# Turning the upper gate frames on VectorE from quarter loads, and adding the gated embedding on GpSimd, in a one-core streaming encoder layer

## The chip, the cores and the metric

The kernel runs on one core of one Trainium2 chip. The metric is the device time of one execution in microseconds (us), taken as a median over runs. The engines are TensorE (PE; its weight loads are PEld), VectorE (DVE), ScalarE (ACT), GpSimd (POOL) and SyncE (SP, which here only issues DMAs). Each engine works through its own queue in order; between queues, semaphores make one instruction wait for another.

## The reference

One layer on 2048 prompt frames and 32 sample frames of 1024 channels, in float32. Cut to what matters:

```python
hn = rmsnorm(h, g_mix)
proj = hn @ w_in                                   # 1024 x 3072
...                                                # yA: gated short convolution, yB: multi-scale pooling
h = h + jnp.concatenate([yA, yB], axis=-1) @ w_out
gate = jax.nn.sigmoid(rmsnorm(h, g_ple) @ w_ple_gate)
h = h + (p @ w_ple) * gate
return rmsnorm(h, g_final)
```

The change concerns the last three lines, the gate stage. The states of the mixers are outputs too; the change does not touch them.

## The kernel before

**Numbers.** Each float32 operand of a matrix product is split into a high part, rounded to the format that PE multiplies (a cast on ACT, L81), and the rest (a subtraction on DVE, L84; the low half). A product is then three matmuls per slice of 128 channels: high by high, high by low, low by high.

**Tiles and products.** Frames come in tiles of 128: tiles 0 to 15 are the prompt, tile 16 is the short tile of 32 sample frames. The gate stage works on pairs of tiles (i, i+1), i = 0, 2, ... 14; "pair 8" is tiles 8 and 9. The even tile is the upper one, the odd the lower. For each pair `seven` (L273) makes seven block products of 12 matmuls each (L185), in three PSUM banks `x_g`, `y_g`, `z_g`, from seven prepared operands: `11` and `12` (the two channel halves of the upper frames), `22`, and the combinations `S1` to `S4` of upper and lower frames. It stands in a scheme of Strassen's kind, so that seven products do the work of eight. The first product of a pair reads `g{i}_11`, the second `g{i}_12`; the last reads `g{i}_22`.

**Preparing a pair.** PE needs the frames with channels on partitions, and `h_d` in DRAM has frames on partitions. `prep_g` makes the operands of pair i+2 while PE works on pair i, in steps that are put between the products of pair i. The *lower* frames are loaded by `by_quarters` (L1512): four DMAs, one per quarter of the channels, each with rows of 1 KB, so that one DVE `STREAM_TRANSPOSE` in place (`turned_here`, L1560) turns the tile. The *upper* frames are loaded whole by one DMA (`load_rows`, L396), brought into another order by two ACT copies `ho` (L1552), and turned by eight PE transposes into a PSUM bank `pth` (L1554); the split and the combinations then read `pth`. `comb` (L1743) adds or subtracts two halves on DVE; `put` splits them.

**After each product.** `gate_ops`: a half of the gate is copied out of PSUM by ACT (`c_g`, L1573), completed by a DVE addition (L1581), put through the sigmoid by ACT (L1582; for the last product of a pair straight from PSUM into `g_g`, L1579), multiplied into the embedding tile `e` by DVE (L1584) and added to `h` by DVE (L1585). There are four such halves in a pair: two for each tile.

**Finishing a tile.** `done_g`: ACT squares and sums `h` (L94, output `junk`), POOL makes the mean (`ms_f`, L73) and its inverse root (`rstd_f`, L77), DVE scales `h` (L1592), and a DMA stores it (L1593, on POOL's queue up to tile 5 and for the short tile, on SP's queue from tile 6). The tiles of pair 12 and before all end so. The last pair is done by `last_pair`, which has an order of its own that is partly written out (`keep_in_program_order`); `done_g(13)` stands within it.

**What sets the order.** Each engine's queue is made by the framework's scheduler from the program's order and the dependences, except for instructions that are kept in program order. A change in what an operation depends on or runs on may thus move others.

The names in the change: `ya`, `xh` are rings of 128x1024 tiles, `ss` and `cmb` rings of smaller ones, `ring4` takes a tile of such a ring, `tiles[i]` gives first row and number of rows, `whole` is a strided view that fits the layout of a tile turned in place.

Of the kernel before, what the change touches and what calls it, by code (L numbers as in the profile page):

```python
# [15 lines left out]
P = 128  # L16
# [20 lines left out]
def trunk(ctx, tc, x_p, x_s, c_conv, c_pool, p_p, p_s, g_mix, w_in, conv_w, conv_b, pool_w,  # L37
# [344 lines left out]
    def ring4(t, name):  # L382
        return t.tile([P, D], F32, tag="t", name=name)
# [920 lines left out]
    with ExitStack() as s2:  # L1304
# [199 lines left out]
        tops, _ = rows_of_weight(ya, "wg_t", g_d, 0)  # L1504
        weight_slot(W, "wg", *PLACES[0])
        weight_parts(W, tops, None, "11", "T1")
        def by_quarters(i):

            r, n = tiles[i]
            t = ring4(ya, f"hn_{i}")  # L1510
            for q in range(4):
                nc.sync.dma_start(t[q * 32:q * 32 + 32].rearrange("p (g c) -> p g c", g=4),  # L1512
                                  h_d[r:r + P, q * 256:q * 256 + 256].rearrange("(g p) c -> p g c", p=32))
            return t
# [13 lines left out]
            bots = rows_of_weight(cmb, "wg_b", g_d, 1, range(2))[0]  # L1528
        with tc.issue_after(embed_weight.ins):
            bots += rows_of_weight(cmb, "wg_b", g_d, 1, range(2, KH))[0]  # L1530
            first_h = load_rows(xh, "hn", 0, h_d)

        rest_e = [*range(EARLY, NT - 2), NT - 1]

# [33 lines left out]
        def gate_ops(h, e, n, name, i):  # L1568
            scale = lambda at: rs_h[:n, i + at[0]:i + at[0] + 1]

            def carry(ps, at):
                t = st.tile([P, NH], F32, tag="t", name=f"c_{name}_{at[0]}{at[1]}")
                carried.append(nc.scalar.copy(t[:n], ps[:n]))  # L1573
                return t

            def out(ps, c, at):
                if c is None:
                    c = st.tile([P, NH], F32, tag="t", name=f"g_{name}_{at[0]}{at[1]}")
                    nc.scalar.activation(c[:n], ps[:n], AF.Sigmoid, scale=scale(at))  # L1579
# [4 lines left out]
                nc.vector.tensor_tensor(ee, ee, c[:n], op=ALU.mult)  # L1584
                nc.vector.tensor_tensor(hh, hh, ee, op=ALU.add)  # L1585

            return carry, out

# [24 lines left out]
        def last_pair(i, A, before):  # L1613
# [118 lines left out]
        def prep_g(i, ahead=False):  # L1732
# [26 lines left out]

            def second():  # L1760
                a21, a22 = lower
                s1 = comb("S1", a21, a22, ALU.add, whole)
# [3 lines left out]
                s3 = comb("S3", whole(a11), a21, ALU.subtract, whole)  # L1766
                put("12", a12)
                put("S2", s2)
                s4 = comb("S4", a12, s2, ALU.subtract)
                put("S1", s1)  # L1770
                put("S3", s3)
                put("S4", s4)
                put("22", a22, whole)

            S[i] = A
# [73 lines left out]
```

## Time and profile before

| | before |
|---|---|
| time, median of 3 runs | 916.7 us (914.71 to 917.25) |
| the profiled execution | 913.25 us |
| its span, first to last instruction | 911.5 us |
| mean granted PE clock | 0.998 |
| PE busy | 894.6 us (98%) |
| DVE busy | 702.9 us (77%) |
| ACT busy | 460.6 us (51%) |
| POOL busy | 149.8 us (16%) |

Times are us from the start of the span unless marked ns. A row of the timeline gives start, length, engine, line, operation, output <- input, the count where several are joined, and in brackets the idle time of that engine just before, with the one that ended it. In rows by groups, busy time and mean length stand behind the first bar, idle time behind the second. The gate stage begins at about 690 us: up to about 732 us PE still makes embedding products, then come the pairs; PE's last matmul ends at 903.77 us.

### The profile page before, as it was taken

The numbers are of one execution on the slowest core, as the hardware profiler recorded it, in microseconds if no ns is written. First come the engines' busy times: TensorE is split into PE (matmuls) and PEld (weight loads), VectorE is DVE, ScalarE is ACT, GpSimd is POOL, SyncE is SP. The second block draws the span as 40 slices with busy tenths as digits, with TensorE's granted clock in tenths as the row PEclk, the third lists the DMA queues.
The fourth block names the chain that finished last, engine by engine and source line by source line (L and its number), as shares of the span: only waits on it lengthen the run. The fifth ranks groups of instructions, "written<-read, shape, count | busy, mean of one in ns | idle before, by whom it ended". The sixth has DMA issues, their size and how long they took to land.

```text
span 911.5 us, 12171 instructions
## 1 busy us (share of the span) xinstructions
PE 894.6 (98%) x4174; PEld 722.5 (79%) x4174; DVE 702.9 (77%) x1158; ACT 460.6 (51%) x834; POOL 149.8 (16%) x290
## 2 busy tenths in 40 slices
PE   8999999999999999999999999999999999999996
PEld 6788888878888887877778887888788888778885
DVE  6899789797993697846667579965666988897885
ACT  7744555455443345533344366544434865565554
POOL 2210121222122114100000020121111211120012
PEclk9999999999999999999999999999999999999999
DMA  8255296748599767567746495887777975575554
GB/s 268 61 187 179 76 269 191 217 151 262 151 328 422 212 201 216 199 216 236 256 129 199 162 318 200 260 245 257 212 267 256 325 257 174 184 237 185 184 192 167
DMA packets 113387, 198.52 MB, mean 218 GB/s; under 512 B 13174, under 2 KB 70062, under 8 KB 112429
## 3 DMA queue, kind: packets, MB, share of 16 engines
q1 hardware_dynamic: 91309, 124.72, 42.5%
q0 software_dynamic: 19568, 68.62, 22.5%
q10 hardware_dynamic: 2448, 4.39, 1.3%
q8 instruction: 33, 0.54, 0.2%
q14 instruction: 29, 0.24, 0.1%
HBM read 132.53 MB, written 65.15 MB: 217 GB/s over the span
## 4 chain that ended last, share of the span: by engine, by line
PE 54%; issue 11%; DMA 10%; DVE 2%; POOL 1%; ACT 1%; POOLq 0%; ACTq 0%; DVEq 0%
PE x_g L185 9%; PE x_o L185 7%; PE z_g L185 5%; DMA raw_zab_0b<-in_w_in_dram 4%; PE x_zab L646 4%; PE x_zbv L646 3%; PE z_o L185 3%; PE x_ch L646 3%; PE y_g L185 2%; PE z_zab L646 2%; PE y_o L185 2%; DMA B<-p_d 2%; PE e L109 2%; PE z_ch L646 1%; PE z_zbv L646 1%
## 5 line engine op out<-in xcount | busy, mean ns | idle before, releaser
L185 PE MATMUL z_o<-wo,y_S 128*128 128x512 f32 x192 | 47.4, 389 | 0.0
L646 PE MATMUL x_zab<-B,w_zab_S 128*128 128x512 f32 x192 | 46.9, 393 | 0.4 <-DVE w_zab_S L84 0.2
L185 PE MATMUL x_o<-wo_T,y_S 128*128 128x512 f32 x192 | 46.3, 390 | 0.6 <-DVE c_o L1319 0.6
L185 PE MATMUL z_g<-wg,g_S 128*128 128x512 f32 x192 | 46.8, 391 | 0.0
L646 PE MATMUL z_zab<-B,w_zab_S 128*128 128x512 f32 x192 | 46.7, 391 | 0.0
L185 PE MATMUL x_o<-wo,y 128*128 128x512 f32 x192 | 45.2, 389 | 0.0
L646 PEld LDWEIGHTS x_zab<-B,w_zab_S 128*128 128x128 f32 x192 | 35.7, 188 | 9.4 <-DVE w_zab_S L84 0.6
L185 PEld LDWEIGHTS x_o<-wo_T,y_S 128*128 128x128 f32 x192 | 35.9, 188 | 8.4 <-DVE c_o L1319 1.0
L185 PEld LDWEIGHTS x_o<-wo,y 128*128 128x128 f32 x192 | 36.1, 188 | 7.7
L646 PEld LDWEIGHTS z_zab<-B,w_zab_S 128*128 128x128 f32 x192 | 35.8, 188 | 7.8 <-DVE w_zab_S L84 0.3
L185 PEld LDWEIGHTS z_o<-wo,y_S 128*128 128x128 f32 x192 | 36.1, 188 | 7.5
L646 PE MATMUL x_ch<-B,w_ch_S 128*128 128x512 f32 x168 | 41.9, 392 | 0.0
L185 PEld LDWEIGHTS z_g<-wg,g_S 128*128 128x128 f32 x192 | 35.8, 188 | 7.5 <-ACT c_g L1573 0.2
L646 PE MATMUL z_ch<-B,w_ch_S 128*128 128x512 f32 x168 | 40.5, 390 | 1.1 <-ACT U L986 1.1
L646 PE MATMUL x_zbv<-B,w_zbv_S 128*128 128x512 f32 x168 | 40.9, 392 | 0.3 <-ACT zs L986 0.3
L646 PE MATMUL z_zbv<-B,w_zbv_S 128*128 128x512 f32 x168 | 40.4, 390 | 0.0
L646 PEld LDWEIGHTS z_ch<-B,w_ch_S 128*128 128x128 f32 x168 | 31.5, 188 | 8.1 <-ACT U L986 1.6
L646 PEld LDWEIGHTS x_zbv<-B,w_zbv_S 128*128 128x128 f32 x168 | 31.3, 188 | 8.1 <-ACT zs L986 0.8
L646 PEld LDWEIGHTS x_ch<-B,w_ch_S 128*128 128x128 f32 x168 | 31.3, 188 | 7.3 <-ACT U L986 0.4
L646 PEld LDWEIGHTS z_zbv<-B,w_zbv_S 128*128 128x128 f32 x168 | 31.5, 188 | 6.5
L81 ACT CAST y_S<-y_fS 128x512 fp32r<-128x512 f32 x28 | 17.0, 619 | 28.1 <-PE x_o L185 12.2
L1319 DVE TENSOR_TENSOR c_o<-x_o,x 128x512 f32<-128x512 f32 x14 | 9.7, 689 | 22.6 <-PE x_o L185 22.6
(552 smaller groups left out, 2285.0 us busy)
## 6 DMA issues: line engine op xcount, KB each, us to landing
wn<-in_w_in_dram SPq DMA_DIRECT2D x24, 512.0 KB, 4.7
y<-y_d SPq DMA_DIRECT2D x16, 512.0 KB, 6.5
p_dT<-T POOLq DMA_DIRECT2D x15, 512.0 KB, 5.2
e<-e_d SPq DMA_DIRECT2D x15, 512.0 KB, 5.0
x<-in_x_prompt_dram SPq DMA_DIRECT2D x14, 512.0 KB, 4.9
B<-p_d POOLq DMA_DIRECT2D x3, 2048.0 KB, 16.8
B<-p_dT POOLq DMA_DIRECT2D x3, 2048.0 KB, 22.8
h_d<-x SPq DMA_DIRECT2D x12, 512.0 KB, 6.3
```

Of the source, the lines that this page charges most:

```text
L81: ins = nc.scalar.copy(hi, src)
L109: nc.tensor.matmul(ps, pps[:, a, k], wp[k][b][:, cs], start=k + q == 0, stop=k == 1 and q == 2)
L185: nc.tensor.matmul(ps[:n], lhs[:, k, a, :n], w[b][:, k], start=start and k + q == 0, stop=k == KH - 1 and q == 2, skip_group_check=True)
L646: nc.tensor.matmul(ps, lhs[:, k, x], b[:, k, y], start=start and k + q == 0, stop=stop and k == KH - 1 and q == 2, skip_group_check=True)
L1319: add = lambda o, a, b: nc.vector.tensor_tensor(o, a, b, op=ALU.add)
```

## The change

Three edits, all in the gate stage:

1. The upper frames are loaded by quarters as the lower ones are (those of pair 0 too, into the ring `xh`), and turned in place by DVE. The copies `ho`, the PE transposes and `pth` are gone for tiles 0, 2, ... 14; the short tile keeps them. Splits and combinations read strided SBUF views.
2. The last addition of the gate, `h += e * gate`, runs on POOL for full tiles (28 additions) and stays on DVE for the short tile.
3. `last_pair` gets a `drain` on POOL, kept in program order. It stands in POOL's queue behind `rstd_f12` and ahead of `ms_f13`.

```diff
-        def by_quarters(i):
+        def by_quarters(i, pool=ya):
             r, n = tiles[i]
-            t = ring4(ya, f"hn_{i}")
+            t = ring4(pool, f"hn_{i}")
...
-            first_h = load_rows(xh, "hn", 0, h_d)
+            first_h = by_quarters(0, xh)
...
-                nc.vector.tensor_tensor(hh, hh, ee, op=ALU.add)
+                (nc.gpsimd if n == P else nc.vector).tensor_tensor(hh, hh, ee, op=ALU.add)
...
+            fixed(nc.gpsimd.drain())
...
-            def comb(q, x, y, op, view=lambda t: t):
-                t = ss.tile([P, KH, P], F32, tag="s", name=f"g{i}_f{q}")
-                nc.vector.tensor_tensor(view(t), x, y, op=op)
+            def comb(q, x, y, op):
+                t = whole(ss.tile([P, KH, P], F32, tag="s", name=f"g{i}_f{q}"))
+                nc.vector.tensor_tensor(t, x, y, op=op)
...
-                got["upper"] = load_rows(ya, "hn", i, h_d) if i else first_h
+                got["upper"] = by_quarters(i) if i else first_h
...
-                a11, a12 = turned(i, got["upper"])
-                put("11", a11)
+                a11, a12 = turned_here(got["upper"])
+                put("11", a11, whole)
```

The other `put` and `comb` lines change in the same way. Lines behind the drain are two higher in the changed kernel (`comb` is L1745 there). The rows of the queues below show what that does to the order at three places. In the names, `g10_11` is operand `11` of pair 10, `hn_10` its upper frames, `e_8`, `h_8` the embedding and the frames of tile 8, `c_g8_01` and `g_g8_10` the gate halves of pair 8; the number behind is the buffer's.

**From pair 8 to pair 10.** DVE's queue before, around the end of pair 8:

```order
L1581 TENSOR_TENSOR c_g8_01_7415<-z_g8_7364,c_g8_01_7415 128x512
L84 TENSOR_TENSOR g10_S4_7454<-g10_fS4_7446,g10_S4_7454 128x4x128
L84 TENSOR_TENSOR g10_22_7457<-hn_11_7395,g10_22_7457 128x4x128
L1584 TENSOR_TENSOR e_9_7360<-e_9_7360,c_g8_11_7472 128x512
L1584 TENSOR_TENSOR e_8_7358<-e_8_7358,c_g8_01_7415 128x512
L1585 TENSOR_TENSOR h_9_7356<-h_9_7356,e_9_7360 128x512
L1585 TENSOR_TENSOR h_8_7354<-h_8_7354,e_8_7358 128x512
L1584 TENSOR_TENSOR e_9_7360<-e_9_7360,g_g8_10_7518 128x512
L1585 TENSOR_TENSOR h_9_7356<-h_9_7356,e_9_7360 128x512
L1581 TENSOR_TENSOR c_g10_00_7561<-y_g10_7547,c_g10_00_7561 128x512
L1592 TENSOR_SCALAR h_8_7354<-h_8_7354,rstd_f8_7526,g_bc_89 128x1024
L1592 TENSOR_SCALAR h_9_7356<-h_9_7356,rstd_f9_7534,g_bc_89 128x1024
```

DVE's queue of the changed kernel at the same place:

```order
L1581 TENSOR_TENSOR c_g8_01_7368<-z_g8_7314,c_g8_01_7368 128x512
L1745 TENSOR_TENSOR g10_fS1_7370<-hn_11_7345 128x512
L1584 TENSOR_TENSOR e_8_7308<-e_8_7308,c_g8_01_7368 128x512
L1584 TENSOR_TENSOR e_9_7310<-e_9_7310,g_g8_10_7458 128x512
L1592 TENSOR_SCALAR h_8_7304<-h_8_7304,rstd_f8_7466,g_bc_89 128x1024
L1560 STREAM_TRANSPOSE hn_10_7350<-hn_10_7350 128x1024
L1592 TENSOR_SCALAR h_9_7306<-h_9_7306,rstd_f9_7474,g_bc_89 128x1024
L84 TENSOR_TENSOR g10_11_7373<-hn_10_7350,g10_11_7373 128x4x128
L1745 TENSOR_TENSOR g10_fS2_7376<-g10_fS1_7370,hn_10_7350 128x512
L1745 TENSOR_TENSOR g10_fS3_7378<-hn_10_7350,hn_11_7345 128x512
L84 TENSOR_TENSOR g10_12_7380<-hn_10_7350,g10_12_7380 128x4x128
```

Before, the low half of `g10_11` stood nine places ahead of the first of these rows; now it stands behind the multiplication by `g_g8_10` and the two scalings L1592, and the transpose of `hn_10` has come between those. On POOL's queue of the changed kernel, the additions of pair 8 and what ends tiles 8 and 9:

```order
L1585 TENSOR_TENSOR h_8_7304<-h_8_7304,e_8_7308 128x512
L1585 TENSOR_TENSOR h_9_7306<-h_9_7306,e_9_7310 128x512
L1585 TENSOR_TENSOR h_8_7304<-h_8_7304,e_8_7308 128x512
L1585 TENSOR_TENSOR h_9_7306<-h_9_7306,e_9_7310 128x512
L73 TENSOR_SCALAR ms_f8_7464<-ssq_f8_7462 128x1
L77 TENSOR_TENSOR rstd_f8_7466<-ms_f8_7464,nhalf_83 128x1
L73 TENSOR_SCALAR ms_f9_7472<-ssq_f9_7470 128x1
L77 TENSOR_TENSOR rstd_f9_7474<-ms_f9_7472,nhalf_83 128x1
```

Only the last four of these stood there before. On PE's queue, the first product of pair 10 (12 matmuls) and two matmuls of its second stood ahead of the last product of pair 8; now they stand behind it.

**From pair 10 to pair 12.** ACT's queue before:

```order
L1552 COPY ho_12_0_7604<-hn_12_7584 128x512
L1552 COPY ho_12_1_7611<-hn_12_7584 128x512
L81 COPY g12_11_7617<-pth_12_0_7603 128x4x128
L81 COPY g12_12_7624<-pth_12_1_7610 128x4x128
L81 COPY g12_S2_7627<-g12_fS2_7620 128x4x128
L81 COPY g12_S1_7632<-g12_fS1_7601 128x4x128
L81 COPY g12_S3_7635<-g12_fS3_7622 128x4x128
```

ACT's queue of the changed kernel:

```order
L1582 ACTIVATE c_g10_11_7586<-c_g10_11_7586,rs_h_88 128x512
L1582 ACTIVATE c_g10_01_7542<-c_g10_01_7542,rs_h_88 128x512
L94 ACTIVATE junk_90,ssq_f10_7636<-h_10_7478 128x1024
L81 COPY g12_11_7547<-hn_12_7524 128x4x128
L81 COPY g12_12_7554<-hn_12_7524 128x4x128
L81 COPY g12_S2_7557<-g12_fS2_7550 128x4x128
```

The square of tile 10 (`ssq_f10`) stood behind the casts of pair 12, and now stands ahead of the first of them.

**From pair 12 to pair 14.** DVE's queue of the changed kernel around the end of pair 12:

```order
L1581 TENSOR_TENSOR c_g12_01_7716<-z_g12_7662,c_g12_01_7716 128x512
L1584 TENSOR_TENSOR e_12_7656<-e_12_7656,c_g12_01_7716 128x512
L1584 TENSOR_TENSOR e_13_7658<-e_13_7658,g_g12_10_7806 128x512
L1560 STREAM_TRANSPOSE hn_14_7698<-hn_14_7698 128x1024
L1592 TENSOR_SCALAR h_12_7652<-h_12_7652,rstd_f12_7814,g_bc_89 128x1024
L84 TENSOR_TENSOR g14_11_7721<-hn_14_7698,g14_11_7721 128x4x128
```

And before, in the same part of the program:

```order
L84 TENSOR_TENSOR g14_11_7801<-pth_14_0_7787,g14_11_7801 128x4x128
L1743 TENSOR_TENSOR g14_fS2_7804<-g14_fS1_7785,pth_14_0_7787 128x512
L1743 TENSOR_TENSOR g14_fS3_7806<-pth_14_0_7787,hn_15_7763 128x512
L84 TENSOR_TENSOR g14_12_7808<-pth_14_1_7794,g14_12_7808 128x4x128
L84 TENSOR_TENSOR g14_S2_7811<-g14_fS2_7804,g14_S2_7811 128x4x128
L84 TENSOR_TENSOR g14_S1_7816<-g14_fS1_7785,g14_S1_7816 128x4x128
L84 TENSOR_TENSOR g14_S3_7819<-g14_fS3_7806,g14_S3_7819 128x4x128
L1743 TENSOR_TENSOR g14_fS4_7814<-pth_14_1_7794,g14_fS2_7804 128x512
L1585 TENSOR_TENSOR h_12_7722<-h_12_7722,e_12_7726 128x512
L1584 TENSOR_TENSOR e_13_7728<-e_13_7728,g_g12_10_7886 128x512
L84 TENSOR_TENSOR g14_S4_7822<-g14_fS4_7814,g14_S4_7822 128x4x128
L84 TENSOR_TENSOR g14_22_7825<-hn_15_7763,g14_22_7825 128x4x128
```

The low half of `g14_11` stood ahead of the last multiplication of pair 12 (by `g_g12_10`); now it stands behind it, the transpose of `hn_14` and the scaling of `h_12`.

More of the change, by code (lines that the diff above doesn't have):

```diff
@@ L1761, in second @@
                 a21, a22 = lower
-                s1 = comb("S1", a21, a22, ALU.add, whole)
-                a11, a12 = turned(i, got["upper"])
-                put("11", a11)
+                s1 = comb("S1", a21, a22, ALU.add)
+                a11, a12 = turned_here(got["upper"])
+                put("11", a11, whole)
                 s2 = comb("S2", s1, a11, ALU.subtract)
-                s3 = comb("S3", whole(a11), a21, ALU.subtract, whole)
-                put("12", a12)
-                put("S2", s2)
+                s3 = comb("S3", a11, a21, ALU.subtract)
+                put("12", a12, whole)
+                put("S2", s2, whole)
                 s4 = comb("S4", a12, s2, ALU.subtract)
-                put("S1", s1)
-                put("S3", s3)
-                put("S4", s4)
+                put("S1", s1, whole)
+                put("S3", s3, whole)
+                put("S4", s4, whole)
                 put("22", a22, whole)
```

## The prediction, made before the changed kernel was run

> **What bounds the kernel now.** I begin with the head of the page, then the table of windows over the last stage, the only one in which the order of instructions changes.
>
> ```profile
> span 911.5 us, 12171 instructions
> PE 894.6 (98%) x4174; PEld 722.5 (79%) x4174; DVE 702.9 (77%) x1158; ACT 460.6 (51%) x834; POOL 149.8 (16%) x290
> ```
>
> TensorE (PE) is busy for 98% of the span. The windows below give, for each stretch, its length and then the busy time of PE, of the weight loads, of VectorE (DVE), ScalarE (ACT) and GpSimd (POOL).
>
> ```profile
> 745.00:770.00 25.00, 25.00 (x118) 20.50 (x116) 20.64 (x31) 14.13 (x26) 3.24 (x7) 1.00 0.50 162
> 770.00:795.00 25.00, 25.00 (x119) 20.05 (x118) 20.73 (x33) 13.08 (x25) 3.90 (x7) 1.00 0.55 181
> 795.00:820.00 25.00, 25.00 (x115) 18.76 (x114) 23.25 (x36) 15.35 (x28) 4.99 (x9) 1.00 0.66 215
> 820.00:845.00 25.00, 25.00 (x116) 20.75 (x115) 19.78 (x31) 12.67 (x23) 1.98 (x4) 1.00 0.49 177
> 845.00:870.00 25.00, 25.00 (x115) 20.57 (x114) 20.35 (x30) 14.63 (x26) 2.81 (x6) 1.00 0.50 176
> 870.00:890.00 20.00, 20.00 (x92) 16.17 (x91) 16.35 (x25) 9.96 (x20) 2.70 (x4) 1.00 0.62 221
> ```
>
> From 745 to 890 us PE has no gap at the full clock. So whatever leaves PE's queue there shortens the kernel by its length, and whatever PE waits for lengthens it by the wait. DVE is idle for 145 − 121.1 = 23.9 us of these 145 us: it is not the bound, but it is not far from it.
>
> **What goes: the transposes on PE.** The chain of waits runs over all eight groups for the upper frames (start, length):
>
> ```profile
> 721.68 0.87 PE pth L1554 x8
> ...
> 834.65 0.87 PE pth L1554 x8
> ...
> 857.11 1.03 PE pth L1554 x8
> ...
> 879.68 1.11 PE pth L1554 x8
> ```
>
> The first six take 0.87 or 0.88 each, the last two are longer: with the six, 5.23 + 1.03 + 1.11 = **7.4 us**, all on the path. (The short tile's two groups stay.) The other costs of this edit, by groups (busy us, mean ns):
>
> ```profile
> L1552 ACT COPY ho<-hn 128x512 f32<-128x512 f32 x16 | 9.3, 619 | 5.3 <-DMA hn<-h_d 5.3
> L1560 DVE STREAM_TRANSPOSE hn<-hn 128x1024 f32<-128x1024 f32 x8 | 9.9, 1237 | 0.1
> L1585 DVE TENSOR_TENSOR h<-h,e 128x512 f32<-128x512 f32 x28 | 18.7, 683 | 0.3
> L1646 POOL TENSOR_TENSOR hg<-h,g_bc 128x512 f32<-128x512 f32 x1 | 1.3, 1310 | 0.1
> ```
>
> ACT loses 9.3 us of copies; it is half idle, so that gains nothing by itself. DVE gets eight more transposes (9.9 us) and gives 28 additions to POOL (18.7 us), 8.8 us less in sum, beside a full PE: nothing by itself. POOL gets 28 additions. The nearest row on POOL, a product of two SBUF tiles of the same size, took 1.31 us, against 0.68 on DVE; so 28 × 1.31 = 36.7 us, on an engine that is 16% busy. What counts is who waits for these additions.
>
> **What is added: waits in queues.** The pair boundary 8→10 before shows every hand-off:
>
> ```profile
> 841.25 0.62 ACT L81 CAST g<-hn 128x512 fp32r<-128x512 f32 x1
> ...
> 841.53 2.88 PE L185 MATMUL x_g<-wq,g 128*128 128x512 f32 x12
> ...
> 842.35 0.68 DVE L84 TENSOR_TENSOR g<-hn,g 128x512 fp32r<-128x512 f32 x1
> ...
> 844.45 0.69 ACT L1579 ACTIVATE g_g<-x_g,rs_h 128x512 f32<-128x512 f32 x1 [1.35 <-PE x_g L185]
> ...
> 845.36 0.68 DVE L1584 TENSOR_TENSOR e<-e,g_g 128x512 f32<-128x512 f32 x1
> ...
> 846.77 0.19 POOL L73 TENSOR_SCALAR ms_f<-ssq_f 128x1 f32<-128x1 f32 x1 [19.47 <-ACT junk L94]
> ...
> 846.93 1.06 ACT L94 ACTIVATE junk<-h 128x1024 bf16<-128x1024 f32 x1 [0.25 <-DVE h L1585]
> ...
> 848.17 0.79 POOL L73 TENSOR_SCALAR ms_f<-ssq_f 128x1 f32<-128x1 f32 x1 [0.58 <-ACT junk L94]
> ...
> 849.04 0.55 POOL L77 TENSOR_TENSOR rstd_f<-ms_f,nhalf 128x1 f32<-128x1 f32 x1
> 849.62 1.28 DVE L1592 SCALAR_TENSOR_TENSOR h<-h,rstd_f,g_bc 128x1024 f32<-128x1024 f32 x1 [0.71 <-POOL rstd_f L77]
> ```
>
> Pair 8's last product ends at 841.53 + 2.88 = 844.41 us, and the sigmoid starts 0.04 later. A hand-off to POOL costs about 0.08 (ACT's 846.93 + 1.06 and its 0.19 of accumulator read, then 848.17), POOL to DVE 0.03. The whole tail of pair 8 lies beside PE, which runs on with pair 10, whose `g10_11` was made long before. In the changed order it isn't. DVE's queue now has, ahead of the low half of `g10_11`, which PE's next product reads: the multiplication by `g_g8_10`, the scaling of `h_8`, the transpose of `hn_10` and the scaling of `h_9`. And POOL's queue has the last addition to `h_9`, which needs that multiplication, ahead of the `rstd_f8` that the scaling of `h_8` waits for. So a closed chain through five in-order queues starts when PE finishes pair 8, and PE can't begin pair 10 until it is through. With E the end of PE's last product of the pair: sigmoid E+0.03 to 0.72; multiplication to 1.44; POOL's addition 1.53 to 2.84; `ms_f8` to 3.11, `rstd_f8` to 3.74; scaling of `h_8` 3.77 to 5.05; transpose to 6.24; ACT's cast to 6.87, DVE's scaling of `h_9` beside it to 7.45; the low half to 8.1. The first two matmuls run on the high half, the other ten (0.227 us each, from 2.72 us for twelve without a gap) after 8.1: the product ends at 10.4 in place of 2.72. **Stall at 8→10: 7.7 us.**
>
> *10→12.* On ACT, the square of `h_10` stands ahead of the cast of `g12_11`, and it waits for POOL's second addition to `h_10`. The z product that opens this ends one product (2.72 us) ahead of E: addition to `c_g10_01` to E−2.0, sigmoid to −1.27, multiplication to −0.55, POOL to +0.85, square and accumulator read 0.95 to 2.1, cast to 2.75. **Stall 2.8 us.**
>
> *12→14.* Here the transpose stands ahead of the scaling of `h_12`, but the low half of `g14_11` stands behind that scaling. The same walk to 5.05, low half to 5.7, ten matmuls to 8.0 against 2.72. **Stall 5.3 us.**
>
> *Earlier pairs.* At 4→6 the transpose of `hn_6` stands behind the multiplication by the gate and ahead of the scaling of `h_4`; the short tile's products, which stand on PE between these pairs, cover most, but its own addition in DVE's queue stands behind all that: 1.1 us, at most 2.7. At 6→8 only the transpose stands between: 0.3, at most 1.5. At 0→2 and 2→4 the order leaves the casts ahead of the waits: 0.
>
> *Loads by quarters.* Two DMA rows: 432 packets of such quarters in a window of 4.6 us, and 420 of whole rows in 5.0 us (packets, MB, share of 16 engines' time).
>
> ```profile
> q1 hardware_dynamic: 432, 0.39, 29.2%
> ...
> q1 hardware_dynamic: 420, 1.56, 86.1%
> ```
>
> A quarter packet takes 0.292 × 4.6 × 16 / 432 = 0.050 us, a 4 KB one 0.861 × 5.0 × 16 / 420 = 0.164; 512 per frame against 128 make 1.6 us of the 16 engines against 1.3. This matters once, for the first upper frames, which are loaded while the DMAs are full and PE waits for `pps`:
>
> ```profile
> 690.00:722.00 32.00, 31.72 (x143) 26.00 (x142) 26.30 (x43) 20.90 (x40) 7.94 (x16) 1.00 0.92 328
> 715.97 5.71 PE L109 MATMUL e<-wq,pps 128*128 128x512 f32 x24 [0.28 <-DMA pps<-pp_d]
> ```
>
> I take 0.3 us (0 to 2, since three more issues on SP's queue may also delay the load behind them). Later quarters land in time: the windows above have DMA at 0.49 to 0.66. The **drain** stands in POOL's queue between `rstd_f12` and `ms_f13`; the row of `rstd_f` gives 0.55 us to wait for, which would lie beside PE: 0, and up to about 3 us if it waited for more than the instruction ahead of it.
>
> **Sum.** Stalls 7.7 + 2.8 + 5.3 + 1.1 + 0.3 + 0.3 = 17.5; minus 7.4 saved: +10.1. On the profiled execution's 913.25 us (span 911.5) this gives 923.4; the median of the runs stands 3.45 higher, so **926.8 us**.
>
> **Rivals.** *A, the other side: the saving alone.* If the transposed frames of the next pair are there before each pair's last product ends, as the copies and casts were before, no boundary stalls, and the time is 916.7 − 7.4 = 909 us. For it: PE has no gap now, and DVE has less to do. Against it: the queue order that I walked. It decides at 7.4 us of stalls in sum: only if two of the three big ones didn't happen would the kernel be faster. Chance 0.09.
>
> *B, GpSimd and VectorE hold each other up.* These rows start within 0.05 us of each other; the same small POOL operation took 0.19 above:
>
> ```profile
> 808.40 1.23 DVE L1592 SCALAR_TENSOR_TENSOR h<-h,rstd_f,g_bc 32x1024 f32<-32x1024 f32 x1
> 808.45 1.24 POOL L73 TENSOR_SCALAR ms_f<-ssq_f 128x1 f32<-128x1 f32 x1 [0.39 <-ACT junk L94]
> ```
>
> So POOL waits for a DVE operation with two SBUF inputs. No row shows the reverse. If it holds, each addition may keep DVE for 1.31 us, 36.7 in all, against DVE's idle 23.9 plus the 8.8 that it gives away: about what it has. One addition more in the way at each of seven boundaries is 7 × 1.31 = 9.2, so 936 us; half of that, 931. The multiplications, the low halves and now the S1 to S4 combinations are all of that kind. But in the three long chains DVE itself waits while POOL adds, so most of the collisions fall into its idle time. Chance 0.17.
> [...]
>
> *C, the stalls are about half as long,* because POOL's addition costs what DVE's does and PE's covers are larger than I walked: 8.7 − 7.4 = +1.3, so 918, about no change. Chance 0.10, half of it within 0.3%.
>
> **How the numbers follow.** The forecast (921 to 931) has 0.60, B 0.17, C 0.10, A 0.09, still slower 0.04. To leave no more than 2 in 10 out, the range goes from C's slower half at 918 to above B's 936: 918 to 938. A measurement of this kernel tells 0.3%, 2.75 us, from no change; faster by more has A's 0.09, within it 0.05, slower 0.86.
>
> **What would show it.** PE idle ahead of the first products of pairs 10, 12 and 14, by about 7.7, 2.8 and 5.3 us, released by DVE's low half (10 and 14) and ACT's cast (12); DVE's L1592 waiting for `rstd_f` and that for L1585 on POOL, 28 rows of about 1.31 us; `pth` only for the short tile. PE without gaps there would refute me and mean A. DVE rows far above 0.7 us beside POOL's additions would mean B; a shorter addition or an earlier sigmoid, C.

## The result and the profile after

| | before | changed |
|---|---|---|
| time, median | 915.71 us (4 runs, 914.32 to 917.25) | 942.47 us (4 runs, 941.55 to 948.2) |
| profiled execution | 913.25 us | 948.2 us |
| span | 911.5 us | 946.4 us |
| mean granted PE clock | 0.998 | 0.982 |

The changed kernel takes 1.031 times as long, 95% interval 1.0289 to 1.033: 26.8 us slower, where 10.1 were forecast, and above the range. The profiled execution is the slowest of its four; its trace has 34.9 us more span to explain. One execution of the kernel before, timed beside runs 9 to 11, took 2320 us and is left out of the median given for it there. Head of the page of the changed kernel:

```profile
span 946.4 us, 12072 instructions
...
PE 902.7 (95%) x4110; PEld 722.6 (76%) x4110; DVE 700.7 (74%) x1138; ACT 454.0 (48%) x818; POOL 189.1 (20%) x318
```

PE has 64 matmuls fewer and is busy 8.1 us longer. Two things need to be found: where PE waits, and why its work takes longer. The windows over the gate stage of the changed kernel show both (columns as before; PEclk is the granted clock, behind the five busy times):

```profile
745.00:770.00 25.00, 21.55 (x89) 17.40 (x88) 14.70 (x21) 12.02 (x21) 7.83 (x9) 0.93 0.66 194
...
795.00:820.00 25.00, 21.76 (x82) 13.96 (x81) 17.60 (x25) 9.17 (x16) 7.56 (x10) 0.86 0.67 203
...
845.00:870.00 25.00, 17.63 (x70) 13.77 (x69) 16.58 (x22) 9.65 (x18) 8.12 (x10) 0.86 0.53 166
...
905.00:920.00 15.00, 10.34 (x34) 7.57 (x33) 11.70 (x16) 6.08 (x10) 4.94 (x5) 0.77 0.36 134
```

Where PE filled every window before, at clock 1.00, these four have gaps and a granted clock of 0.77 to 0.93. The gaps of PE between pairs, from the timeline (in brackets the idle time ahead, and who ended it):

```profile
759.35 4.51 PE L185 MATMUL x_g<-wq,g 128*128 128x512 f32 x12 [3.45 <-DVE c_g L1581]
808.26 0.73 PE L185 MATMUL x_g<-wg,g 128*128 128x512 f32 x2 [1.20 <-ACT g L81]
810.18 1.07 PE L185 MATMUL x_g<-wg,g 128*128 128x512 f32 x2 [1.19 <-DVE g L84]
812.10 1.97 PE L337 MATMUL x_gl<-wg,gl_a 128*64 128x512 f32 x4 [0.84 <-DVE c_gl L1601]
835.38 0.73 PE L185 MATMUL x_g<-wg,g 128*128 128x512 f32 x2 [0.74 <-ACT g L81]
837.60 4.16 PE L185 MATMUL x_g<-wg,g 128*128 128x512 f32 x10 [0.97 <-DVE g L84]
865.00 4.74 PE L185 MATMUL x_g<-wg,g 128*128 128x512 f32 x12 [7.37 <-ACT g L81]
888.67 1.05 PE L185 MATMUL x_g<-wg,g 128*128 128x512 f32 x2 [2.58 <-ACT g L81]
913.14 1.22 PE L185 MATMUL x_g<-wg,g 128*128 128x512 f32 x2 [3.52 <-ACT g L81]
915.51 4.45 PE L185 MATMUL x_g<-wg,g 128*128 128x512 f32 x10 [1.15 <-DVE g L84]
```

By pair these are 3.45 at 0→2, 3.23 at 4→6, 1.71 at 6→8, 7.37 at 8→10, 2.58 at 10→12 and 4.67 at 12→14: 23.0 us. The first row also shows the second thing: 12 matmuls take 4.51 us, and in the seventh 4.74, where before they took 2.88.

**The budget.** From the end of the embedding products to PE's last matmul: 171.3 us before (732.45 to 903.76), 201.6 now (737.81 to 939.41). The difference of 30.3 is 23.0 of gaps, minus 6.5 for seven `pth` groups, plus 13.8 that is left for the same matmuls, which took longer. The starts of the rows behind the six boundaries show about 12 of the 13.8 as matmuls at half speed; the rest is the tail of the last matmul ahead of each of ten gaps, which without a gap overlaps the next (a product lasts 2.88, and the next starts 2.72 behind its start). Ahead of that, the embedding products took 2.0 us more, of which two waits of 0.52 and 2.37, less one of 0.28 before and the eighth `pth` group of 0.87, make 1.7. And the changed part was reached 3.4 us later, after work that the diff doesn't touch. 30.3 + 2.0 + 3.4 is 35.7; 0.8 came back behind the last matmul, which leaves the 34.9. The 3.4 can't be put down to the change: the first embedding product started at 707.4 us before, at 710.7 here, at 708.2 in runs 1 and 2 below, and at 710.4 and 707.6 in runs 3 and 4, which have both edits. Run 4, with the same loads, also has 0.60 us of waits among the embedding products where this trace has 2.89. So up to 6 us of the 34.9 may belong to this one execution, which took 5.7 us more than the median; why is open.

**The walk at 8→10**, from the timeline of the changed kernel. PE's last product of pair 8 ends at 857.63:

```profile
857.67 0.69 ACT L1579 ACTIVATE g_g<-x_g,rs_h 128x512 f32<-128x512 f32 x1 [0.70 <-PE x_g L185]
857.77 1.26 POOL L1585 TENSOR_TENSOR h<-h,e 128x512 f32<-128x512 f32 x1 [1.93 <-DVE e L1584]
858.39 1.19 DVE L1584 TENSOR_TENSOR e<-e,g_g 128x512 f32<-128x512 f32 x1 [0.70 <-ACT g_g L1579]
...
859.65 1.26 POOL L1585 TENSOR_TENSOR h<-h,e 128x512 f32<-128x512 f32 x1 [0.63 <-DVE e L1584]
...
861.86 1.28 DVE L1592 SCALAR_TENSOR_TENSOR h<-h,rstd_f,g_bc 128x1024 f32<-128x1024 f32 x1 [2.28 <-POOL rstd_f L77]
...
863.06 1.24 DVE L1560 STREAM_TRANSPOSE hn<-hn 128x1024 f32<-128x1024 f32 x1
...
864.33 1.14 ACT L81 CAST g<-hn 128x512 fp32r<-128x512 f32 x2 [2.23 <-DVE hn L1560]
...
865.38 0.69 DVE L84 TENSOR_TENSOR g<-hn,g 128x512 fp32r<-128x512 f32 x1
```

It is the chain that was forecast, link by link: sigmoid, multiplication, GpSimd's addition, `rstd`, scaling, transpose, cast, low half. The low half ends 8.44 us after PE's product, 8.1 were forecast. PE's wait ended 1.07 us sooner, with the cast, as the first two matmuls don't read the low half. The third row holds a surprise: the multiplication took 1.19 in place of 0.68. GpSimd's addition, which had started first, ended at 859.03, and the multiplication 0.55 behind it.

**The clock.** Windows of the changed kernel, cut around the product of 4.74 us:

```profile
860.00:864.90 4.90, 0.00 (x0) 0.00 (x0) 3.04 (x3) 1.93 (x6) 3.21 (x5) 0.66 0.20 79
864.90:867.00 2.10, 2.00 (x4) 1.28 (x5) 2.10 (x4) 0.87 (x3) 0.00 (x0) 0.50 0.53 207
867.00:869.70 2.70, 2.70 (x10) 2.09 (x10) 2.70 (x6) 1.36 (x3) 0.00 (x0) 0.74 1.02 303
869.70:875.00 5.30, 5.30 (x25) 4.38 (x24) 3.25 (x5) 2.40 (x4) 0.22 (x1) 1.00 1.07 261
```

The window that lies wholly within the slow stretch, 864.90 to 867.00, shows 0.50: half clock. So a mean of 0.66 over 4.90 us is full clock for 1.57 and half clock for 3.33, and the clock fell at 861.57; a mean of 0.74 over 2.70 puts its return at 868.40. That is 6.83 us at half clock, and part of it falls on PE's work. The same working on windows around the other gaps gives 3.4 us at 0→2, 6→8 and 10→12, and 6.8 at 4→6 and 12→14. What sets these lengths, and when the clock falls, is not shown. The two gaps of 0.74 and 0.97 at 6→8 were enough (ten matmuls in 4.16, where run 4 below has 2.56 at full clock), while the 2.37 us gap among the embedding products cost no clock (1.00 from 719 to 728). Nor does the length of the gaps alone decide: run 5 below has gaps of 0.74 and 0.95 at the same place, and full clock behind them:

```profile
832.93 2.57 PE L185 MATMUL x_g<-wg,g 128*128 128x512 f32 x10 [0.95 <-DVE g L84]
```

And the same program loses more or less in different executions: one of the four of run 5 took 934.71 us at a mean granted clock of 0.992, the other three 937.83 to 943.21 at 0.985.

### The profile page after: what moved, and what is told of

Same layout as the page of the kernel before. It is cut to its first block, busy times and chain, and to the rows that moved or that the text cites. A ratio compares the mean times of both kernels' runs of the same rounds, so it can differ in the third digit from the quotient of the medians.

```text
span 946.4 us, 12072 instructions
## 1 busy us (share of the span) xinstructions
PE 902.7 (95%) x4110; PEld 722.6 (76%) x4110; DVE 700.7 (74%) x1138; ACT 454.0 (48%) x818; POOL 189.1 (20%) x318
## 4 chain that ended last, share of the span: by engine, by line
PE 43%; DMA 14%; issue 12%; DVE 7%; POOL 2%; ACT 2%; SPq 0%; POOLq 0%; ACTq 0%; DVEq 0%
PE x_g L185 7%; PE x_o L185 5%; PE x_zab L646 4%; DMA raw_zab_0b<-in_w_in_dram 4%; PE x_zbv L646 3%; PE x_ch L646 3%; DMA gs<-in_w_ple_gate_dram 3%; PE z_g L185 3%; PE z_o L185 2%; PE z_zab L646 2%; PE y_g L185 2%; DMA hn<-h_d 2%; DMA B<-p_d 2%; PE e L109 1%; PE z_ch L646 1%
## 5 line engine op out<-in xcount | busy, mean ns | idle before, releaser
L1585 POOL TENSOR_TENSOR h<-h,e 128x512 f32<-128x512 f32 x28 | 41.3, 1480 | 82.1 <-DVE e L1584 71.0
L185 PE MATMUL x_g<-wg,g 128*128 128x512 f32 x96 | 33.3, 497 | 18.7 <-ACT g L81 15.4
L185 PEld LDWEIGHTS x_g<-wg,g 128*128 128x128 f32 x96 | 22.5, 245 | 28.3 <-ACT g L81 17.6
L646 PEld LDWEIGHTS x_zab<-B,w_zab_S 128*128 128x128 f32 x192 | 35.7, 188 | 9.6 <-ACT V L986 0.8
L1592 DVE SCALAR_TENSOR_TENSOR h<-h,rstd_f,g_bc 128x1024 f32<-128x1024 f32 (+1 forms) x15 | 19.2, 1281 | 24.7 <-POOL rstd_f L77 24.7
```

The costliest lines, as they stand in the source:

```text
L185: nc.tensor.matmul(ps[:n], lhs[:, k, a, :n], w[b][:, k], start=start and k + q == 0, stop=k == KH - 1 and q == 2, skip_group_check=True)
L646: nc.tensor.matmul(ps, lhs[:, k, x], b[:, k, y], start=start and k + q == 0, stop=stop and k == KH - 1 and q == 2, skip_group_check=True)
L1585: (nc.gpsimd if n == P else nc.vector).tensor_tensor(hh, hh, ee, op=ALU.add)
L1592: nc.vector.scalar_tensor_tensor(h[:n], h[:n], rf[:n], g_bc[:n], op0=ALU.mult, op1=ALU.mult)
```

## The experiments

The forecast left 16.7 us unexplained in sum. **Theory S** puts the loss on edit 1: transposes and loads of the upper frames that come late. **Theory G** puts it on edit 2: GpSimd's additions, as a longer link or because they hold VectorE up. Later expectations name the theories that they test. The kernel before was timed beside each group of runs: 914.08 us with the first four, 913.79 with the next four, then 914.99 (three), 914.35 (one) and 914.75 (the last two).

**1. Turning alone.** Edit 1; VectorE adds as before, no drain.

```diff
-                (nc.gpsimd if n == P else nc.vector).tensor_tensor(hh, hh, ee, op=ALU.add)
+                nc.vector.tensor_tensor(hh, hh, ee, op=ALU.add)
...
-            fixed(nc.gpsimd.drain())
```

> Only the first edit: upper frames by quarters and turned by VectorE; the last addition stays on VectorE, no drain. Theory S (stalls from the late transposes, each followed by about 2 us of half clock): the transposes of hn_10, hn_12 and hn_14 still stand behind the gate's last operations in VectorE's queue, so the stalls stay, at 8 to 10 about 7 to 8 us, at 10 to 12 about 2, at 12 to 14 about 4 to 5, with half clock after each: 932 to 942 us. Theory G (GpSimd's additions make the loss, by the longer hand-off and by holding VectorE up): the loss goes with them, 912 to 920 us.

935.32 us, ratio 1.0233 (1.0217 to 1.0248): 21 us slower. PE waited 2.35 us at 0→2, 8.50 at 8→10, 1.51 at 10→12 and 5.44 at 12→14, and the clock fell again (a mean of 0.987; the twelve matmuls behind the wait at 0→2 took 4.33). So S: the stalls at the boundaries need no GpSimd. That refutes how I had written them, as chains through GpSimd's addition; with VectorE's the chain is even longer at 8→10 and 12→14.

**2. Additions alone.** Edit 2; the upper frames as before.

```diff
-                nc.vector.tensor_tensor(hh, hh, ee, op=ALU.add)
+                (nc.gpsimd if n == P else nc.vector).tensor_tensor(hh, hh, ee, op=ALU.add)
```

> Only the second edit: the last addition of the gate on GpSimd, upper frames turned by TensorE as before. Theory S: the casts of the next pair stand ahead of the chain in every queue, so TensorE does not wait for it: 914 to 920 us. Theory G: most of the 27 us, 930 us or more, with VectorE operations longer than 1 us beside GpSimd's additions.

923.08 us, ratio 1.0099 (1.0082 to 1.0116): 9 us slower, in neither theory's range. Its longest wait of PE is on the way through the copies `ho`:

```profile
PE pth L1554 <- ACT ho L1552: 3.8, 3, 2.4
```

**3. No drain.** The changed kernel without the line of the drain.

> The changed kernel without the drain; the order of all other instructions is the same. Both theories: the drain waits for one operation of 0.55 us beside TensorE, so 941 to 943 us, no difference. If the drain waited for more, 1 to 3 us faster. The trace is also a second look at the changed order: the stalls at 8 to 10, 10 to 12 and 12 to 14 should again be about 7.4, 2.6 and 4.7 us.

945.37 us (940.87 to 951.18), ratio 1.0346 (1.0298 to 1.0393); its gaps at 8→10, 10→12 and 12→14 are 7.38, 2.58 and 3.52 + 1.15. The drain costs nothing that this shows.

**4. Filled gaps.** The changed kernel, with 30, 8 and 16 matmuls that nobody reads behind pairs 8, 10 and 12.

```diff
+            idle = tbank(f"idle_{i}") if i >= 8 else None
+            for c in range({8: 30, 10: 8, 12: 16}.get(i, 0)):
+                w = W["T4"][0]
+                tc.keep_in_program_order(nc.tensor.matmul(idle, w[:, c % KH, :P], w[:, c % KH], start=True, stop=True))
```

> The changed kernel with extra matmuls whose result nobody reads, on TensorE between the last product of a pair and the first of the next: 30 at 8 to 10, 8 at 10 to 12, 16 at 12 to 14, each 0.227 us, so 6.8, 1.8 and 3.6 us, less than the idle time there (7.4, 2.6, 4.7). Theory S with the clock: TensorE keeps full clock, the first 12 matmuls behind the gap take 2.7 us in place of 4.7 at 8 to 10, and the kernel becomes 4 to 6 us faster though TensorE does 12 us more: 936 to 938 us. Rival (the long matmuls behind a stall come from something else, such as operands still being made): they stay long, 942 us or slower.

939.22 us (938.26 to 940.3), ratio 1.0275 (1.0254 to 1.0295), 6.2 below run 3 beside it. From the timeline of this kernel, at 8→10:

```profile
852.29 6.96 PE L1820 MATMUL idle<-wq 128*128 128x512 f32 x30
859.88 0.73 PE L185 MATMUL x_g<-wg,g 128*128 128x512 f32 x2 [0.62 <-ACT g L81]
860.99 2.56 PE L185 MATMUL x_g<-wg,g 128*128 128x512 f32 x10 [0.39 <-DVE g L84]
```

The 54 matmuls are 12.7 us more work for PE, and the kernel is no slower: the ten matmuls behind this gap run at full clock (2.56; the granted clock is 1.00 from 845 to 870). The clock's share of the loss is shown by itself, some 3 us against the changed kernel and 6 against run 3 for three of the six boundaries.

**5. Stores on another queue.** Why do the transposes stand so late? Rows of SP's queue show when the upper frames of pair 10 are asked for. The changed kernel (L1512 are the quarters, L1593 the stores of tiles 6 and 7):

```profile
841.23 0.79 SPq L1512 DMA_DIRECT2D hn<-h_d  x2
842.99 4.92 SPq L1593 DMA_DIRECT2D out_dram<-h  x2
847.95 3.19 SPq L1512 DMA_DIRECT2D hn<-h_d  x6
```

The kernel before, at the same place (L396 is the whole upper tile):

```profile
826.64 2.36 SPq L1593 DMA_DIRECT2D out_dram<-h  x2
829.05 0.42 SPq L396 DMA_DIRECT2D hn<-h_d  x1
```

A store waits for VectorE's scaling, and as the queue is in order, the loads behind it wait too (between 830 and 866 us the changed kernel's SP queue stood 18.0 us for the scalings of four stores): the last upper quarters go out at 851 us, 6.5 us ahead of the end of pair 8, where the whole tile went out at 829, 15.4 ahead of it. A second reason is the ring `ya`: a tile turned in place stays in use up to its last split, where the copies `ho` freed it early. This run moves the stores, and the next three also give the upper frames room.

```diff
-            (nc.sync if 6 <= i < NT - 1 else nc.gpsimd).dma_start(rows_of(y_p, y_s, r, n), h[:n])
+            nc.gpsimd.dma_start(rows_of(y_p, y_s, r, n), h[:n])
```

> The changed kernel with the stores of tiles 6 to 13 on GpSimd's DMA queue in place of SP's; nothing else. Theory Q (the next upper frames are loaded late, because their loads stand on SP's queue behind stores that wait for the scaling, and so their transposes come late): the queue orders change, and the transposes of hn_10, hn_12 and hn_14 now stand ahead of the last multiplication of the pair before; ACT still squares one tile ahead of the casts, so stalls of about 3 us stay at each of the three: 8 to 10 falls from 7.4 to about 3.4, 12 to 14 from 4.7 to about 3, in all 933 to 938 us. Rival (the lateness comes from VectorE's load, not from the loads of frames): no change, 941 to 945 us.

938.45 us (934.71 to 943.21), ratio 1.0269 (1.0232 to 1.0306). This is just above the 933 to 938 expected. The gap at 8→10 fell from 7.37 to 3.16, and the 4.67 at 12→14 to 2.58; the gaps at the other boundaries stayed, and one of 1.45 came in at the end, behind the drain (see run 8).

**6 to 8. A buffer of their own for the upper frames,** made by joining two 2 KB buffers `qa` into one of 4 KB, which earlier stages use as well.

```diff
-        qa, xh, ya, cmb = (pool(*a) for a in (("qa", 2), ("xh", 4), ("ya", 5), ("cmb", 8)))
+        qa, xh, ya, cmb = (pool(*a) for a in (("qa", 1), ("xh", 4), ("ya", 5), ("cmb", 8)))
...
-                got["upper"] = by_quarters(i) if i else first_h
+                got["upper"] = by_quarters(i, qa) if i else first_h
```

Run 6 has this with turning alone; run 7 the stores of run 5 as well; run 8 all edits with both.

> The first edit alone (as in the run before with turning only, 935.3 us), with the upper frames in a buffer of their own (4 KB a partition, made of two buffers of 2 KB of which the short tile alone had use) and not in the ring that they share with the lower frames and the embedding tiles. Theory Q: the tile is loaded when its last user in the pair before is done, so the waits at 0 to 2 and 4 to 6 go, but the stores on SP's queue still delay the load at 8 to 10: 920 to 930 us. Rival (buffers don't matter): 935 us.

> The first edit alone, with both: the upper frames in a buffer of their own and the stores on GpSimd's queue. Theory Q: all transposes and low halves stand ahead of the last multiplication of the pair before; a wait of about 1.3 us at 8 to 10 behind the sigmoid and short ones elsewhere; the 7.4 us of the transposes on TensorE are gained: 907 to 914 us, the first version under the kernel before. Rival (turning on VectorE costs too much there): 918 us or more.

> All edits of the changed kernel, with the upper frames in a buffer of their own and the stores on GpSimd's queue. Theory Q: transposes, casts and low halves stand ahead of the last multiplication everywhere, so GpSimd's additions delay only what is off the path: 907 to 914 us. Theory G (GpSimd's additions hold VectorE up or make it late by themselves): 8 us or more above the run with the first edit alone and the same two mends.

932.53, 924.4 and 931.23 us; ratios 1.0192 (1.0158 to 1.0227), 1.0112 (1.0097 to 1.0127) and 1.0185 (1.0168 to 1.0202). All missed 907 to 914 or 920 to 930. In run 7 the gaps at 8→10 and 10→12 are down to 1.83 and 2.23, but the pairs begin 6.8 us later than before: joining the buffers costs the stages ahead. In run 8 POOL shows a new wait:

```profile
901.28 0.63 POOL L1600 DMA_DIRECT2D out_dram<-h  x1
911.99 0.18 POOL L73 TENSOR_SCALAR ms_f<-ssq_f 128x1 f32<-128x1 f32 x1 [10.08 <-issue]
```

That is the drain, behind a DMA that POOL has just issued: 10.08 us, and PE then waits 5.81. In run 5 it was 7.97 and 1.45. In the kernel as changed no such DMA stands near it. Run 8 is 6.8 us above run 7, less than the 8 that theory G asked for, and this wait alone could make most of it.

**9. Room in another way.** Turning alone, stores as in run 5; the odd embedding tile is loaded as two halves into the two `qa` buffers, which leaves a slot of `ya` to the upper frames.

```diff
-            e = [load_rows(ya, "e", i + b, e_d) for b in range(2)]
+            e = [load_rows(ya, "e", i, e_d), [qa.tile([P, NH], F32, tag="q", name=f"e_{i + 1}_{half}") for half in range(2)]]
+            for half, t in enumerate(e[1]):
+                nc.sync.dma_start(t, e_d[(i + 1) * P:(i + 2) * P, half * NH:half * NH + NH])
```

> The first edit alone (turning on VectorE, additions on VectorE), with two mends that leave the earlier stages as they were: the embedding tile of the odd frames is loaded as two halves into the two 2 KB buffers that only the short tile used, so that the shared ring of five has one tile less to hold, and the stores of tiles 6 to 13 go out on GpSimd's queue. Theory Q (late loads of the upper frames, from the shared ring and from SP's queue, make the late transposes): from 6 to 8 on TensorE has no wait at the pair boundaries; left are about 1 us before the pairs, 4 at 0 to 2 and 1 to 2 at 4 to 6, against 7.4 gained: 911 to 919 us. Rival (turning on VectorE is late by itself): 925 us or more.

915.94 us (914.38 to 917.58, 10 runs), ratio 1.0012 (0.9997 to 1.0027). Of the 21.2 us that turning cost in run 1 over the kernel before beside it, about 1 is left, and no gap is left at 8→10, 10→12 and 12→14, with the same steps on VectorE. The last loads for pair 10 go out some 10 us ahead of the end of pair 8, and the transpose of its upper frames now runs at 840.83, 5.3 us ahead of that end (846.14); in the changed kernel it ran at 863.06, 5.4 behind it.

**10. The same with the additions on GpSimd** (no drain).

> The first and second edits with the same two mends, without the drain (with the stores on GpSimd's queue it waited 8 to 10 us for a DMA). Theory Q: also here the casts stand ahead of the last multiplication from 6 to 8 on; GpSimd's additions then cost only at 0 to 2 and 4 to 6: 914 to 923 us. Theory G (the additions cost by themselves, as the 8 to 9 us of the run with them alone suggest): 8 us or more above the run with turning alone and the same mends.

926.75 us, ratio 1.0128 (1.0104 to 1.0152): 10.8 above run 9, and above the 914 to 923 of theory Q. The part of G that concerns edit 2 holds.

**11. Control:** the kernel before with the stores moved as in run 5.

> The kernel before with the stores of tiles 6 to 13 on GpSimd's queue: a control for the mend by itself. TensorE has no gap at the boundaries of the kernel before, so the mend can gain nothing there: 913 to 917 us. If it gains or loses more than 2 us, the runs with the mend have to be read against this one.

915.05 us, ratio 1.0001 (0.9986 to 1.0017). Moving the stores by itself is worth nothing.

**12. Additions that nobody waits for.** Run 9's kernel, VectorE adding, and beside it 28 GpSimd additions of the same size whose result is not used, each started by the multiplication that would start the real one.

```diff
-                nc.vector.tensor_tensor(ee, ee, c[:n], op=ALU.mult)
+                gated = nc.vector.tensor_tensor(ee, ee, c[:n], op=ALU.mult)
...
+                if n == P:
+                    behind(nc.gpsimd.tensor_tensor(unread, g_bc[:, :NH], g_bc[:, NH:], op=ALU.add), gated, "as late as the addition")
```

> The run with turning on VectorE and both mends (915.9 us), in which VectorE still makes all additions, plus 28 additions of the same size on GpSimd, each started by the same multiplication as the real one, of a constant tile with itself into a tile that nobody reads. The order of the other engines is unchanged. Theory L (GpSimd's additions cost because h is finished later: 1.3 us and two hand-offs more ahead of the squares, scalings, stores and of the buffers' release): nobody waits for these, so 915 to 918 us. Theory P (they cost because they hold VectorE's operations up while they read): VectorE's operations with two inputs in SBUF become longer, by 6 to 8 us in sum, and the time rises to 920 us or more, toward the 926.8 us of the run with the real additions and the same mends.

933.43 us, ratio 1.0207 (1.0179 to 1.0234): 17.5 above run 9 by the medians, 18.1 when each is taken against the kernel before beside it. Groups of this kernel:

```profile
L1590 POOL TENSOR_TENSOR unread<-g_bc 128x512 f32<-128x512 f32 x28 | 45.6, 1628 | 70.6 <-DVE e L1587 70.0
L1588 DVE TENSOR_TENSOR h<-h,e 128x512 f32<-128x512 f32 x28 | 35.9, 1299 | 3.3 <-issue 3.2
```

and the same group of run 9:

```profile
L1586 DVE TENSOR_TENSOR h<-h,e 128x512 f32<-128x512 f32 x28 | 18.6, 681 | 1.9 <-issue 1.8
```

One collision in run 12, from the timeline:

```profile
856.17 1.32 POOL L1590 TENSOR_TENSOR unread<-g_bc 128x512 f32<-128x512 f32 x1 [7.84 <-DVE e L1587]
...
856.54 1.49 DVE L84 TENSOR_TENSOR g_S<-g_fS,g_S 128x512 fp32r<-128x512 f32 x1
```

VectorE's subtraction began 0.37 behind GpSimd's addition and ended at 858.03, 0.54 behind its end; the multiplication in the walk at 8→10 ended 0.55 behind GpSimd's. The subtraction took 1.49, the next one, with no GpSimd operation beside it, 0.68: this collision cost VectorE 0.81 us. This is the reverse case that no row of before showed. There is one thing in POOL's queue that does wait for these additions, the `rstd_f` behind them; but VectorE's scaling waits for it no longer than in run 9 (7.8 us in sum against 7.9). Since VectorE here makes its own 28 additions too, the 17.5 us are the price of collisions in this kernel, and not of the edit.

**13 and 14. The first pairs the old way.** Run 9 had saved 7.4 us of `pth` and yet only equalled the kernel before. Its gaps are at the first pairs: 1.26 us among the embedding products, 0.39 at 4→6, 0.85 at the short tile, 1.05 at 6→8, and at 0→2, behind a load on VectorE's side:

```profile
746.65 1.25 DVE L1561 STREAM_TRANSPOSE hn<-hn 128x1024 f32<-128x1024 f32 x1 [4.23 <-DMA hn<-h_d]
...
755.38 4.48 PE L185 MATMUL x_g<-wq,g 128*128 128x512 f32 x12 [1.78 <-DVE c_g L1582]
```

Run 13 takes run 9's kernel and loads pair 0's upper frames whole, turned by PE; run 14 does so for pairs 0 and 2.

```diff
-            first_h = by_quarters(0, xh)
+            first_h = load_rows(xh, "hn", 0, h_d)
...
+                if i == 0:
...
+                    a11, a12 = turned(i, got["upper"])
+                    put("11", a11)
```

> Turn-only with both mends, but pair 0's upper frames loaded whole and turned by TensorE as before the change; the other pairs take quarters and VectorE. Theory L (the waits of pair 0 at its e products come from its quarter loads, which stand among other loads): the 1.26 us wait at the e products is gone, one pth group (0.87 to 1.1 us) comes back, and the 1.78 us wait at 0 to 2 with its 1.7 us of half clock stays: 914 to 916. Rival R (that wait comes from a busy VectorE or ScalarE, not from the loads): the wait stays beside the pth group, 916.5 to 918.

> The same with pairs 0 and 2 both loaded whole and turned by TensorE. Theory L: the wait at 0 to 2 goes as well, with its 3.4 us period at half clock, and a second pth group comes back (about 1 us): 911 to 914, under the kernel before. Rival R: the wait at 0 to 2 stays near 1.8 us: 916 to 919.

Run 13: **909.37 us** (908.41 to 912.38, 6 runs), ratio 0.9944 (0.9923 to 0.9965), 5.4 us under the kernel before. Run 14: 913.66 us (911.83 to 915.37, 12 runs), ratio 0.9985 (0.9972 to 0.9998). Run 13 is better than theory L had it, because the waits at 0→2, 4→6 and 6→8 went as well. For 0→2 SP's queue says why. In run 9, and then in run 13, at the loads of pair 2:

```profile
732.57 4.75 SPq L1513 DMA_DIRECT2D hn<-h_d  x8
```

```profile
725.91 8.29 SPq L1513 DMA_DIRECT2D hn<-h_d  x8
```

The next loads on the queue go out 6.7 us earlier in run 13, and the transpose no longer waits for them. It is not the number of issues: four for pair 0 took 2.86 us, the one 0.36. In run 9 the queue stood 7.2 us ahead of them, until VectorE had used a tile of the weights for the last time (L1793, which is L1814 in run 13, where it stood 0.3 us ahead of the first load and 3.3 ahead of a later one). That ran behind the transpose of pair 0's upper frames and the operands made from them, at 731.83; in run 13 the first of these subtractions ran ahead of the operands, at 725.14, as in the kernel before (723.42, its loads at 724.17). In the changed kernel it was 735.17, and the loads 735.95. In run 13 PE's only gap from the embedding products on is

```profile
PE x_gl L337 <- DVE c_gl L1602: 0.4, 1, 0.4
```

Run 14's expectation held in its number and not in its reason: 0→2 had nothing left to give, and run 14 has gaps of 0.74 at 4→6, 0.84 at the short tile and 1.04 at 6→8 beside the second `pth` group. Run 9 has nearly the same (0.39, 0.85, 1.05), run 13 only 0.40 at the short tile. What brings these is open.

## Why the prediction was wrong, step by step

Two steps failed. The sum counted each gap at its own length and put nothing for the matmuls behind it; and the walk held the loads to be in time, with no stall at 0→2. In the trace the change cost 34.9 us where 10.1 were forecast. Of these 24.8, 13.8 are matmuls that took longer, 5.8 are gaps at the pairs (23.0, of which 17.2 were forecast), 2.6 the embedding products, and 2.6 lie outside the changed part.

- **What goes, 7.4 us: right.** 6.5 in the pairs and 0.87 at the embedding products; runs 9 and 13 show that it can be had.
- **Stalls of 7.7, 2.8 and 5.3 us: right in size** (7.37, 2.58 and 4.67) and in the order of links. **Their cause was only half told.** The walk took the queue order as given, and charged the stall to the links. Run 1 has these stalls without GpSimd in the chain, and run 9 has none of them. What differs is where the transpose and the low half stand in VectorE's queue: ahead of the end of the pair before in run 9, behind it in the changed kernel.
- **"Later quarters land in time", and with it "At 0→2 and 2→4 … 0": this step failed, at 0→2.** VectorE stood still for the load of pair 2:

```profile
750.81 1.25 DVE L1560 STREAM_TRANSPOSE hn<-hn 128x1024 f32<-128x1024 f32 x1 [5.15 <-DMA hn<-h_d]
```

  PE then waited 3.45 us. I argued from the DMA engines' busy share of 0.49 to 0.66. The engines had room; the queue that issues the loads had not. It stood 7.5 us for a tile that the weights held until VectorE's L1793, which turning pair 0 on VectorE had moved back from 723.42 to 735.17. Run 13, with pair 0's upper frames as before, has no wait at 0→2. I had looked only for the delay of three more issues, and priced it at 0 to 2 us for the embedding products alone. These gave 2.89 us of gaps in this trace (0.60 in run 4), 0.3 were forecast. 4→6 and 6→8 gave 3.23 and 1.71 in place of 1.1 and 0.3, above the 2.7 and 1.5 named as the most.
- **At 8→10 the loads were late in another way.** The last quarter of pair 10 was issued at 850.7 and took at most 3.8 us to land, so it was there about 3 us before pair 8 ended, as I had said. But the transpose stood in VectorE's queue behind the scaling of `h_8`. Runs 5, 9 and 11 bear on this together: moving the stores and freeing a slot brings the loads and the transposes forward, and takes turning from 21.2 us over the kernel before to about 1; moving the stores alone is worth nothing to the kernel before. The mends change the time of the loads and the order of the queue at once. That the scheduler puts a transpose late because its load is late is the likely link, and no run shows it by itself.
- **Missing from the sum: the clock, about 12 of the 13.8 us.** At each of the six boundaries the clock fell to half for 3.4 or 6.8 us, and PE worked in part of that time. Gaps of 25.9 us in all and 13.8 of clock, less 7.4 saved, are 32.3, near the trace's 34.9; the rest is mostly the 3.4 us ahead of the changed part. Rival C, stalls of half the size, falls with these.
- **Rival B, GpSimd and VectorE: a real cost, and not where I weighed it.** I said that most collisions would fall into VectorE's idle time. Run 12 puts a price of 17.5 us on 28 more additions whose result nobody reads; run 10 puts 10.8 and run 2 9.0 on the real ones. In the changed kernel itself, whose VectorE was busy for 120 of the 175 us from 745 to 920, the groups of VectorE are stretched less:

```profile
L1585 POOL TENSOR_TENSOR h<-h,e 128x512 f32<-128x512 f32 x28 | 41.3, 1480 | 82.1 <-DVE e L1584 71.0 <-DMA hn<-h_d 11.0
...
L1745 DVE TENSOR_TENSOR g_fS<-hn,hn 128x512 f32<-128x512 f32 x7 | 5.9, 837 | 0.0
```

  An addition took 1.48 on GpSimd, 1.31 were forecast. The costs don't add up: 21.2 (run 1) and 9.0 (run 2) make 30.2, the whole change 26.8. How run 10's 10.8 divides isn't settled: from 735 to 905 us its VectorE waits 22 us for `rstd_f` where run 9 waits 8, which is the longer link, and its two-input operations take about 8 us longer in sum.
- **Rival A** had the saving alone, 7.4 us. Run 13 shows 5.4 of it, without edit 2 and with one `pth` group kept; that its 909.37 us meets A's 909 is chance, since the kernel before took 914.75 beside it and not 916.7.
- **The drain: 0, right** where it stands; behind a DMA of POOL's own it waited 7.97 us (run 5) and 10.08 (run 8).

## What to carry to other kernels

When a tile is turned in place, ask how long its buffer is now held and what stands ahead of its load in the queue that issues it; a free DMA engine is no answer to either (here the engines' share was 0.52 to 0.67 from 745 to 890 us, and the queue stood 7.5 us for one tile). Put the clock into the sum beside the gaps: in the changed kernel's trace matmuls at half clock cost some 12 us over six boundaries, about 2 at each, while gaps of 0.74 and 0.95 in run 5 cost no clock, and the four executions of run 5 had mean clocks of 0.985 to 0.992. Before work goes from VectorE to GpSimd to relieve it, count how often the two would run at once: here 28 additions of 0.68 us cost 9 to 11 us when moved.

## What the runs showed of the hardware

- In the changed kernel's trace the granted clock fell to 0.50 at six boundaries with gaps of 1.7 to 7.4 us in sum, for 3.4 us at three of them and for 6.8 at the others; a gap of 2.37 us elsewhere in that trace, and gaps of 0.74 and 0.95 in run 5 at 6→8, brought none. In run 4, with 30 matmuls that nobody reads at 8→10 and gaps of 0.62 and 0.39 left, it was 1.00 from 845 to 870 us.
- Two VectorE operations with two SBUF inputs that started 0.62 and 0.37 us behind a GpSimd addition of two SBUF tiles ended 0.55 and 0.54 behind its end, after 1.19 us (changed kernel, 8→10) and 1.49 (run 12) in place of 0.68. VectorE's 28 additions took 1299 ns in the mean in run 12, against 681 in run 9.
- In runs 5 and 8 the drain on GpSimd stood behind a DMA that its own queue had just issued, and the next operation waited 7.97 and 10.08 us; without the drain (run 10) it waited 2.05 us, and for ScalarE.
